# Order of the wide and narrow matmuls in joined products, and joined output tiles 4 to 6 in the mixers

## The chip, the cores and the metric

The kernel runs on one core of a Trainium2 chip. The metric is the device time of one execution in microseconds (us). Five engines of the core matter: TensorE (PE in the profile; its weight loads are shown apart as PEld), VectorE (DVE), ScalarE (ACT), GpSimd (POOL) and SyncE (SP, which issues DMAs). Each works through its instructions in the order in which the program gave them, and semaphores hold an instruction back until its operands are there.

## The reference

The reference is an encoder trunk of four layers over 256 positions of 1024 features. Each layer is a half-step SwiGLU feed-forward network (FFN), a token mixer, and a second FFN, each with a root-mean-square norm ahead of it and behind it:

```python
for i in range(DEPTH):
    g = norm_g[i]
    x = x + 0.5 * rms_norm(swiglu(rms_norm(x, g[0]), ff1_w_in[i], ff1_w_out[i]), g[1])
    h = rms_norm(x, g[2])
    m = mixer_a / mixer_b / mixer_c (h, ...)      # i mod 3
    x = x + rms_norm(m, g[3])
    x = x + 0.5 * rms_norm(swiglu(rms_norm(x, g[4]), ff2_w_in[i], ff2_w_out[i]), g[5])
```

with `swiglu(h) = (silu(gate) * up) @ w_out`, where `gate` and `up` are the halves of `h @ w_in`, of 2816 columns each. Mixer A (layers 0 and 3) is chunked attention with a position bias, mixer B (layer 1) a gated MLP that mixes positions, mixer C (layer 2) differential attention. Each mixer ends in a product with a 1024 x 1024 matrix `w_o`.

## The kernel before

**Numbers in two parts.** Each float32 operand of the large products is held as a high part, rounded to the format that TensorE takes, and a low part, what is left over. A product of weights W and activations X is formed as `Wh*Xh + Wh*Xl + Wl*Xh`. Activations lie transposed (features on the 128 partitions, 256 positions, `S`, along the row), so that a block of 128 x 128 weights times 128 features is a matmul of 256 columns.

**Two ways to multiply.** `product` (L162 to L172) issues three matmuls of 256 columns for each weight block k. `product2` (L174 to L183) takes the high weights against the high and the low activations side by side, one matmul of 512 columns (L177, the wide ones), and then the low weights against the high activations, 256 columns (L179, the narrow ones), which add onto the first half of the same accumulator. All wide matmuls of a call come first, then all narrow ones. A call has eight blocks, or fewer where a weight piece ends inside an output tile. The two halves of the accumulator have to be added afterwards; that is what "joined" means here.

**Where they are used.** An FFN takes its input projection in 11 steps of four weight pieces. The first step has a form of its own (L510 or L529); the other ten call `product2` four times each through `project_apart`. The output product has eight tiles d = 0 to 7 of 22 blocks each; the 22 blocks are cut at the borders of the weight pieces (eight blocks each) into three or four calls. Tiles 0 to 6 use `product2` (25 calls), tile 7 uses `product`. A mixer ends in `project_out`: its tiles 0 to 3 are formed together (L653), tiles 4 to 7 one after the other with `product` (L169), 24 matmuls each. So there are 40 + 25 calls of `product2` in each of the eight FFNs and none in a mixer.

**What happens to an output tile.** `Branch.tile_done` lets ScalarE square the tile (L376, `sq`, or `ysq` for tile 0) and write it times its gain to `yg` (L377); VectorE adds the square to `ysq` (L387). For a joined tile `Branch.joined` comes first: ScalarE copies the second half out of the accumulator (L366, `share`), VectorE adds it to the first half into `yg` (L367), and the square and the gain then read `yg`. After tile 7 TensorE sums the squares over the features (L239): first `ysq` (tiles 0 to 6), then, after four filling matmuls (L449 or L451, early parts of the next stage's first product, by the class `Ahead`), tile 7's `sq`. ScalarE and VectorE make a reciprocal root of it (L247, L249), eight more filling matmuls run beside that, and L254 spreads it over the partitions. Then the residual is updated and the next norm begins. In a mixer the inputs of those filling matmuls that come from `yg` are made late (`YLATE`): three tiles' parts after tile 4 and two after tile 5, each with a ScalarE instruction (L410) and a VectorE instruction (L411).

**The weight stream.** Weights come in pieces of eight blocks, two to a DMA of 1 MB on SyncE's queue, into three buffers. ScalarE rounds a piece to its high part (L127), VectorE subtracts it to get the low part (L130). Eight pieces are held in each form. `W.done` gives a piece back and issues the split of the piece eight further on; a split's VectorE half is issued only with the next split, or by `W.settle`. In a mixer's output one split is issued after tiles 0 to 3 and one after each of the tiles 4, 5 and 6; at tile 7 the stream is held (`W.hold`) until the next norm.

**Order.** The program fixes the order on TensorE, VectorE and ScalarE by hand: it is the order of the calls. Accumulators (`pair()`) come from three pairs of PSUM banks, used in turn.

Of the kernel before, what the change touches and what calls it, by code (L numbers as in the profile page):

```python
# [18 lines left out]
S = 256  # L19
DEPTH = 4  # L20
KD = D // P
# [35 lines left out]
def encoder_trunk_kernel(  # L57
# [14 lines left out]
    nc = tc.nc  # L72
# [90 lines left out]
    W = Stream()  # L163

    def product(o, wh, wl, x, ks, at, start, stop):

        for i, k in enumerate(ks):
            for m, (w_, low) in enumerate(((wh, 0), (wh, 1), (wl, 0))):
                nc.tensor.matmul(  # L169
                    o, w_[:, at + i, :], x(k)[:, low, :], start=(start and i == 0 and m == 0),  # L170
                    stop=(stop and k == ks[-1] and m == 2),
                )  # L172

    def product2(o, wh, wl, x, ks, at, start, stop):  # L174

        for i, k in enumerate(ks):
            nc.tensor.matmul(o, wh[:, at + i, :], x(k), start=(start and i == 0), stop=False, skip_group_check=True)  # L177
        for i, k in enumerate(ks):
            nc.tensor.matmul(  # L179
                o[:, 0:S], wl[:, at + i, :], x(k)[:, 0, :], start=False, stop=(stop and k == ks[-1]),  # L180
                skip_group_check=True,
            )

    def pair():
        return pp.tile([P, 2, 512], F32, tag="pp", name="pp_t")
# [215 lines left out]
    class Ahead:  # L401
# [7 lines left out]
        def parts(self, dst, src, scale):  # L409
            nc.scalar.activation(dst[:, 0, :], src, AF.Copy, scale=scale)  # L410
            nc.vector.scalar_tensor_tensor(  # L411
                dst[:, 1, :], src, scale, dst[:, 0, :].bitcast(F32), op0=ALU.mult, op1=ALU.subtract
            )
# [82 lines left out]
    def blocks(piece):  # L496
        return [part.rearrange("p (k c) -> p k c", k=KD) for part in piece]
# [40 lines left out]
    def project_apart(n, between, finish, most=2):  # L538

        for i in range(4):  # L540
            if i % 2 == 0:
                ps = pair()
            wh, wl = blocks(W.peek())
            product2(ps[:, i % 2, :], wh, wl, lambda k: n.x[:, k], range(KD), 0, True, True)
            if i % 2 == 1:
                finish(i // 2, ps)
            between(i)
            W.done(1, most)
# [93 lines left out]
    def project_out(parts, l, between, ahead):  # L642

        br = Branch(g_sb[:, l, 3, :], None, ahead)
        ws = [blocks(W.peek(e)) for e in range(4)]
        os = [ps[:, e, 0:S] for ps in (pair(), pair()) for e in range(2)]
        for k, low in ORDER:
            if not low:
                between(k)
            x = parts(k)  # L650
            for (wh, wl), o in zip(ws, os):
                for part in (wh,) if low else (wh, wl):
                    nc.tensor.matmul(  # L653
                        o, part[:, k, :], x[:, int(low), :], start=(k == 0 and part is wh and not low),
                        stop=(k == KD - 1 and low), skip_group_check=True,
                    )
            if low and k >= PUMP:
                W.pump(1)
        W.settle()
        for d in range(4):  # L660
            br.tile_done(d, os[d])
        W.done(4, 1)
        for d in range(4, KD):
            o = pair()[:, 0, 0:S]
            wh, wl = blocks(W.peek())
            product(o, wh, wl, parts, range(KD), 0, True, True)
            if d == KD - 1:
                W.hold()
                W.done()
            br.tile_done(d, o)  # L670
            if d < KD - 1:
                W.done(1, 1)
        return br.finish()

    def joined(early, outs):
# [157 lines left out]
    def mixer_a(l, i, update):  # L833
# [86 lines left out]

        late = attention(n, softmax, transposes, v_done, mix)
        return project_out(parts, l, between, ahead)

    def mixer_b(l, i, update):
# [94 lines left out]
        def between(k):  # L1019
# [3 lines left out]
            if k == 3:  # L1023
                split(3)
                nc.scalar.preload_act_table(AF.Sqrt)

        return project_out(lambda k: op[:, k], l, between, ahead)

    def mixer_c(l, i, update):
# [144 lines left out]
        ss = small.tile([P, 16], F32, tag="sso", name="sso", bufs=1)  # L1174
        late = attention(n, softmax, transposes, v_done, mix, prepare, lambda: split(0))
        return project_out(parts, l, between, ahead)

    mixers = (mixer_a, mixer_b, mixer_c)
# [87 lines left out]
```

## Time and profile before

| | |
|---|---|
| Time, median of 3 runs | 1955.42 us (1954.46 to 1955.93) |
| Profiled execution: time, span of its instructions | 1959.09 us, 1957.4 us |
| Mean granted clock of TensorE | 0.997 |
| Wide matmuls of `product2` (L177) | 2560 + 672 + 560 = 3792 |
| Narrow matmuls of `product2` (L179) | 3792 |
| Moved from HBM | 347.44 MB, 178 GB/s over the span |

Times in the profile are those of one profiled execution, from the start of its first instruction. The duration of one matmul includes its way through the array, and the next begins before it has ended: the distance between two starts says more than the duration. The same holds, by about 0.1 us, for instructions of ScalarE and VectorE that stand in a full queue. In rows of the timeline the columns are start, time covered, engine, line, operation, output and inputs, shapes and count; in brackets stands the idle time ahead of it and what ended that.

### The profile page before, as it was taken

Reading aid. Unit: us, or ns where it says so; the run is one execution under the profiler, and the core shown is the slowest. Engines: PE = TensorE matmul, PEld = TensorE weight load, DVE = VectorE, ACT = ScalarE, POOL = GpSimd, SP = SyncE. Lnnn points to the kernel's source line nnn. Section 1 sums busy time; section 2 is a strip of 40 time slices with the busy share of each in tenths; the row PEclk is TensorE's granted clock in tenths of the full one; section 3 lists DMA queues with packets and bytes.
Section 4 is the critical chain, followed back from the end, with each engine's and each line's share of the span. In section 5 each row is a group of like instructions: output and inputs, shape, how many; then the busy total and the mean of one; then the engine's idle time right before and its main releaser. Section 6 shows DMA issues by size and latency. Waiting matters only on the chain.

```text
span 1957.4 us, 30171 instructions
## 1 busy us (share of the span) xinstructions
PE 1941.6 (99%) x12435; PEld 1750.1 (89%) x12435; DVE 1385.1 (71%) x1905; ACT 1177.5 (60%) x1826; POOL 6.7 (0%) x21
## 2 busy tenths in 40 slices
PE   9999999999999999999999999999999999999998
PEld 8888999888988888888988899988898889999887
DVE  6775767866777667867676668786667666868763
ACT  6655657656555555756565655675656565666652
POOL 0000000000000000000000000000000000000000
PEclk9999999999999999999999999999999999999999
DMA  7555534654455553554455535255546454535551
GB/s 260 201 187 200 188 108 153 233 188 180 173 194 188 199 158 147 207 196 177 159 207 190 198 145 181 109 196 194 191 151 214 176 204 159 197 125 182 200 201 44
DMA packets 50473, 350.43 MB, mean 179 GB/s; under 512 B 5760, under 2 KB 6016, under 8 KB 9120
## 3 DMA queue, kind: packets, MB, share of 16 engines
q1 hardware_dynamic: 48096, 341.86, 48.9%
q10 hardware_dynamic: 2160, 6.52, 0.9%
q8 instruction: 97, 1.59, 0.3%
q0 software_dynamic: 80, 0.13, 0.0%
q14 instruction: 40, 0.33, 0.0%
HBM read 347.44 MB, written 1.05 MB: 178 GB/s over the span
## 4 chain that ended last, share of the span: by engine, by line
PE 97%; DVE 1%; DMA 1%; ACT 0%; issue 0%; ACTq 0%; SPq 0%; DVEq 0%
PE pp_t L177 45%; PE pp_t L179 23%; PE pp_t L529 8%; PE pp_t L169 6%; PE pp_t L510 3%; PE pp_t L694 3%; PE pp_t L653 2%; DMA w_raw<-in_w 1%; PE pp_t L734 1%; PE pp_t L451 1%; PE pst_t L766 1%; PE pst_t L451 1%; PE pst_t L239 1%; PE pst_t L254 1%; PE pp_t L449 0%; PE pp_t L888 0%
## 5 line engine op out<-in xcount | busy, mean ns | idle before, releaser
L130 DVE TENSOR_TENSOR w_lo<-w_raw,w_hi 128x1024 fp32r<-128x1024 f32 (+1 forms) x649 | 774.7, 1217 | 57.9 <-ACT w_hi L127 57.8
L127 ACT CAST w_hi<-w_raw 128x1024 fp32r<-128x1024 f32 (+1 forms) x649 | 667.6, 1046 | 122.4 <-PE pp_t L177 84.1
L177 PE MATMUL pp_t<-xp,w_hi 128*128 128x512 f32 x2560 | 642.5, 393 | 0.0
L177 PEld LDWEIGHTS pp_t<-xp,w_hi 128*128 128x128 f32 x2560 | 460.2, 189 | 82.4
L179 PEld LDWEIGHTS pp_t<-xp,w_lo 128*128 128x128 f32 x2560 | 349.2, 190 | 25.1
L179 PE MATMUL pp_t<-xp,w_lo 128*128 128x256 f32 x2560 | 356.8, 282 | 0.0
L600 DVE TENSOR_TENSOR gu<-pp_t,share 128x512 f32<-128x512 f32 x160 | 110.6, 691 | 209.4 <-ACT share L599 209.3
L599 ACT COPY share<-pp_t 128x512 f32<-128x512 f32 x160 | 93.5, 585 | 179.3 <-PE pp_t L179 179.3
L177 PE MATMUL pp_t<-h,w_hi 128*128 128x512 f32 x672 | 175.7, 393 | 0.0
L177 PE MATMUL pp_t<-l,w_hi 128*128 128x512 f32 x560 | 148.8, 394 | 0.0
L570 ACT ACTIVATE gs<-gs 128x512 f32<-128x512 f32 x88 | 55.7, 632 | 141.0 <-DVE gs L569 141.0
L177 PEld LDWEIGHTS pp_t<-h,w_hi 128*128 128x128 f32 x672 | 117.7, 189 | 17.9
L529 PE MATMUL pp_t<-xp,w_hi 128*128 128x256 f32 x832 | 124.3, 288 | 1.7 <-ACT xp L315 1.4
L177 PEld LDWEIGHTS pp_t<-l,w_hi 128*128 128x128 f32 x560 | 100.0, 189 | 20.1 <-DVE l L579 2.9
L529 PEld LDWEIGHTS pp_t<-xp,w_hi 128*128 128x128 f32 x832 | 111.5, 193 | 4.2 <-ACT xp L315 1.6
L179 PEld LDWEIGHTS pp_t<-h,w_lo 128*128 128x128 f32 x672 | 97.7, 190 | 10.3
L367 DVE TENSOR_TENSOR yg<-pp_t,share 128x256 f32<-128x256 f32 x56 | 23.8, 424 | 110.3 <-ACT share L366 110.3
L179 PE MATMUL pp_t<-h,w_lo 128*128 128x256 f32 x672 | 100.6, 282 | 0.0
L179 PEld LDWEIGHTS pp_t<-l,w_lo 128*128 128x128 f32 x560 | 79.6, 190 | 6.1
L179 PE MATMUL pp_t<-l,w_lo 128*128 128x256 f32 x560 | 84.8, 282 | 0.0
L315 ACT ACTIVATE xp<-xr,g_sb 128x256 fp32r<-128x256 f32 x96 | 44.8, 503 | 58.6 <-DVE xr L482 56.5
L529 PE MATMUL pp_t<-xp,w_lo 128*128 128x256 f32 x416 | 73.8, 284 | 0.0
(198 smaller groups left out, 2297.3 us busy)
## 6 DMA issues: line engine op xcount, KB each, us to landing
w_raw<-in_w SPq DMA_DIRECT2D x322, 1024.0 KB, 4.8
l<-in_a_bias ACTq DMA_DIRECT2D x8, 512.0 KB, 8.8
w_raw<-in_w SPq DMA_DIRECT2D x3, 512.0 KB, 8.8
out_y<-xr SPq DMA_DIRECT2D x4, 256.0 KB, 2.1
xr<-in_x_t SPq DMA_DIRECT2D x2, 384.0 KB, 7.0
w_raw<-in_w SPq DMA_DIRECT2D x2, 256.0 KB, 4.7
l<-in_b_ws ACTq DMA_DIRECT2D x1, 512.0 KB, 5.4
l<-in_b_ln_g ACTq DMA_DIRECT2D x1, 512.0 KB, 9.3
```

Of the source, the lines that this page charges most:

```text
L127: nc.scalar.copy(hi[:, cols], raw[:, cols])
L130: nc.vector.tensor_tensor(lo[:, cols], raw[:, cols], hi[:, cols].bitcast(F32), op=ALU.subtract)
L169: nc.tensor.matmul(o, w_[:, at + i, :], x(k)[:, low, :], start=(start and i == 0 and m == 0), stop=(stop and k == ks[-1] and m == 2),)
L177: nc.tensor.matmul(o, wh[:, at + i, :], x(k), start=(start and i == 0), stop=False, skip_group_check=True)
L179: nc.tensor.matmul(o[:, 0:S], wl[:, at + i, :], x(k)[:, 0, :], start=False, stop=(stop and k == ks[-1]), skip_group_check=True,)
L315: nc.scalar.activation(self.h[:, k, :], xr[:, k, :], AF.Copy, scale=gain[:, k:k + 1])
L510: nc.tensor.matmul(o, part[:, k, :], n.x[:, k, int(low), :], start=((k, low) == JOIN[0] and i == 2 and part is ws[i][0]), stop=((k, low) = ...
L529: nc.tensor.matmul(o, part[:, k, :], n.x[:, k, low, :], start=(at == 0), stop=(at == 3 * KD - 1))
L570: nc.scalar.activation(gs, gs, AF.Silu)
L599: nc.scalar.copy(share, ps[:, :, S:2 * S])
L600: nc.vector.tensor_tensor(at.t[:, e], ps[:, :, 0:S], share, op=ALU.add)
L694: nc.tensor.matmul(self.ps[:, t, :], xs[:, kk, t * P:(t + 1) * P], ws, start=((kk, low) == self.order[0] and ws is wh and not (t == 0 and ...
```

## The change

`product2` keeps a switch that turns with every call. One call issues its wide matmuls (high weights) first and its narrow ones (low weights) after, as before; the next issues the narrow ones first and the wide ones after. The flags that begin and end the accumulation go to whichever matmul is first and last. In `project_out` tiles 4, 5 and 6 are formed by `product2` and finished by `joined`; tile 7 stays with `product`.

```diff
+    turn = [False]
+
     def product2(o, wh, wl, x, ks, at, start, stop):
-        for i, k in enumerate(ks):
-            nc.tensor.matmul(o, wh[:, at + i, :], x(k), start=(start and i == 0), stop=False, skip_group_check=True)
-        for i, k in enumerate(ks):
-            nc.tensor.matmul(
-                o[:, 0:S], wl[:, at + i, :], x(k)[:, 0, :], start=False, stop=(stop and k == ks[-1]),
-                skip_group_check=True,
-            )
+        turn[0] = not turn[0]
+        for low in (False, True) if turn[0] else (True, False):
+            for i, k in enumerate(ks):
+                nc.tensor.matmul(
+                    o[:, 0:S] if low else o, (wl if low else wh)[:, at + i, :], x(k)[:, 0, :] if low else x(k),
+                    start=(start and i == 0 and low != turn[0]), stop=(stop and k == ks[-1] and low == turn[0]),
+                    skip_group_check=True,
+                )
...
         for d in range(4, KD):
-            o = pair()[:, 0, 0:S]
+            o = pair()[:, 0, :]
             wh, wl = blocks(W.peek())
-            product(o, wh, wl, parts, range(KD), 0, True, True)
-            if d == KD - 1:
+            if d < KD - 1:
+                product2(o, wh, wl, parts, range(KD), 0, True, True)
+                br.joined(d, o)
+                W.done(1, 1)
+            else:
+                product(o[:, 0:S], wh, wl, parts, range(KD), 0, True, True)
                 W.hold()
                 W.done()
-            br.tile_done(d, o)
-            if d < KD - 1:
-                W.done(1, 1)
+                br.tile_done(d, o[:, 0:S])
```

## The prediction

> **What bounds the kernel now.** I read the page first: busy shares, granted clock, the chain that ended last, the costliest groups.
>
> ```profile
> PE 1941.6 (99%) x12435; PEld 1750.1 (89%) x12435; DVE 1385.1 (71%) x1905; ACT 1177.5 (60%) x1826; POOL 6.7 (0%) x21
> ...
> PEclk9999999999999999999999999999999999999999
> ...
> PE 97%; DVE 1%; DMA 1%; ACT 0%; issue 0%; ACTq 0%; SPq 0%; DVEq 0%
> ...
> L177 PE MATMUL pp_t<-xp,w_hi 128*128 128x512 f32 x2560 | 642.5, 393 | 0.0
> ...
> L179 PE MATMUL pp_t<-xp,w_lo 128*128 128x256 f32 x2560 | 356.8, 282 | 0.0
> ```
>
> TensorE is the chain and its matmuls follow each other without a gap, so what counts is the distance from start to start, not the 393 and 282 ns, which overlap. The chain in order of time gives it.
>
> ```profile
> 34.57 1.84 PE pp_t L177 x8
> ...
> 137.93 1.84 PE pp_t L177 x8
> ...
> 202.51 8.84 PE pp_t L694 x39
> ...
> 299.68 11.52 PE pp_t L169 x96
> ```
>
> Unmixed runs: 8.84/39 = 0.2267 us for 512 columns, 11.52/96 = 0.1200 us for 256. Eight of each would be 2.773 us. The first two rows are the first and last of 38 evenly spaced products: (137.93 - 34.57)/37 = 2.7935 us. So a product pays **0.020 us** for going from one width to the other and back. The timeline shows on which side:
>
> ```profile
> 61.39 1.12 PE L179 MATMUL pp_t<-xp,w_lo 128*128 128x256 f32 x8
> ...
> 62.34 2.00 PE L177 MATMUL pp_t<-xp,w_hi 128*128 128x512 f32 x8
> ...
> 64.19 1.11 PE L179 MATMUL pp_t<-xp,w_lo 128*128 128x256 f32 x8
> ```
>
> Start to start, eight wide ones take 1.85 us instead of 1.81, eight narrow ones 0.95 instead of 0.96.
>
> **The change, part 1: the order in `product2`.** It runs 40 + 25 times per FFN, 520 times in all. With every other call begun low, two calls share one round trip: half of them go. By piece lengths 14 of an FFN's 25 output calls are full and 11 short (2, 4 or 6 blocks); so 432 full calls at 0.020, and 88 short ones at half that by my choice (0 to 0.020 possible): 9.5 us of switching, of which **-4.7 us** goes (-4.3 to -5.2).
>
> A call begun low needs the low weights 1.8 us earlier, but pieces are split eight ahead, over 20 us; and it frees the high half up to 0.95 us later, for which ScalarE's next split waits. Behind that split on ScalarE stands a `share` copy that waits for a product's end anyway, and three PSUM pairs give it two more pairs' time: nothing. One small wait shrinks, in the third output call of each FFN:
>
> ```profile
> 140.56 1.77 PE L177 MATMUL pp_t<-l,w_hi 128*128 128x512 f32 x6
> 142.16 0.40 PE L179 MATMUL pp_t<-l,w_lo 128*128 128x256 f32 x2
> ```
>
> Six take 1.60 us, 0.21 over 6 x 0.231: they wait for the last hidden blocks' low part. By the parity of the calls (65 in an FFN, 3 now in a mixer) the four FFNs of layers 1 and 3 begin this call low, and reach that part later: 4 x 0.21 = 0.8 at most, 0 if their narrow matmuls wait instead; I take **-0.4**.
>
> **Part 2: tiles 4 to 6 of the four mixers.** TensorE saves 2.88 - 2.79 = 0.09 us on each, 0.28 per mixer. But each tile's result now takes ScalarE `share`, VectorE add, ScalarE square, ScalarE scale one after the other. The FFN's output shows these:
>
> ```profile
> 143.13 0.37 ACT L366 COPY share<-pp_t 128x256 f32<-128x256 f32 x1 [0.43 <-PE pp_t L179]
> ...
> 143.54 0.42 DVE L367 TENSOR_TENSOR yg<-pp_t,share 128x256 f32<-128x256 f32 x1 [0.53 <-ACT share L366]
> ...
> 144.00 0.42 ACT L376 ACTIVATE ysq<-yg 128x256 f32<-128x256 f32 x1 [0.49 <-DVE yg L367]
> ...
> 144.45 0.51 ACT L377 ACTIVATE yg<-yg,g_sb 128x256 f32<-128x256 f32 x1
> 144.86 0.49 ACT L410 ACTIVATE ahead<-xr,g_sb 128x256 fp32r<-128x256 f32 x1
> ```
>
> 1.73 us of ScalarE's order. Hidden in an FFN, where a tile is 22 blocks long; a mixer's has 8. ScalarE there, mixer of layer 0:
>
> ```profile
> 301.98 1.10 ACT L127 CAST w_hi<-w_raw 128x1024 fp32r<-128x1024 f32 x1
> 302.91 0.45 ACT L376 ACTIVATE sq<-pp_t 128x256 f32<-128x256 f32 x1
> ...
> 303.55 1.38 ACT L410 ACTIVATE ahead<-yg,g_sb 128x256 fp32r<-128x256 f32 x3
> 304.75 1.11 ACT L127 CAST w_hi<-w_raw 128x1024 fp32r<-128x1024 f32 x1
> 305.68 0.46 ACT L376 ACTIVATE sq<-pp_t 128x256 f32<-128x256 f32 x1
> ...
> 306.31 0.99 ACT L410 ACTIVATE ahead<-yg,g_sb 128x256 fp32r<-128x256 f32 x2
> 307.12 1.12 ACT L127 CAST w_hi<-w_raw 128x1024 fp32r<-128x1024 f32 x1
> 308.36 0.38 ACT L376 ACTIVATE sq<-pp_t 128x256 f32<-128x256 f32 x1
> ...
> 309.00 1.05 ACT L127 CAST w_hi<-w_raw 128x1024 fp32r<-128x1024 f32 x1
> 311.24 0.38 ACT L376 ACTIVATE sq<-pp_t 128x256 f32<-128x256 f32 x1 [1.19 <-PE pp_t L169]
> ```
>
> No idle from tile 0 to tile 6: it is full, and has only 0.3 us before tile 6's square (308.36; the cast ended its turn at 308.05) and 1.3 before tile 7's (311.24; 309.93). Today square and scale take 0.64 (302.91 to 303.55); new, 1.09 more per tile, 1.14 with the somewhat later end of an instruction in a full queue. VectorE adds to it:
>
> ```profile
> 305.36 1.22 DVE L130 TENSOR_TENSOR w_lo<-w_raw,w_hi 128x1024 fp32r<-128x1024 f32 x1
> ...
> 307.74 1.22 DVE L130 TENSOR_TENSOR w_lo<-w_raw,w_hi 128x1024 fp32r<-128x1024 f32 x1
> 308.87 0.41 DVE L387 TENSOR_TENSOR ysq<-ysq,sq 128x256 f32<-128x256 f32 x1
> 309.21 2.35 DVE L130 TENSOR_TENSOR w_lo<-w_raw,w_hi 128x1024 fp32r<-128x1024 f32 x2
> ```
>
> The adds of tiles 5 and 6 stand behind a weight split, moved with the rest. Tile 4: the cast of 304.75 comes 1.14 later, at 305.89. Tile 5: `share` at 306.83 could let the add go at 307.25, but the split of 305.36, now 306.47, holds VectorE to 307.60: 1.14 + 0.33, and the cast of 307.12 comes at 309.72. Tile 6: `share` at 310.65; the split of 307.74 holds VectorE from 310.29 to 311.43, again about 0.32 lost; the add ends at 311.85, square at 312.30, the cast of 309.00 comes at 312.74, tile 7's square at 313.67, **2.43 late**. TensorE, after tile 7:
>
> ```profile
> 311.04 0.50 PE L239 MATMUL pst_t<-ones,ysq 128*128 128x1 f32 x4
> ...
> 311.96 0.50 PE L239 MATMUL pst_t<-ones,sq 128*128 128x1 f32 x4
> ```
>
> It comes to the first sums at 310.76 and waits for tile 6's square sum (today 308.87, then about 312.32 to 312.75): start 312.78, 1.9 us idle. Everything behind waits in TensorE's order: four filling matmuls, then the second sums, which need tile 7's square: 313.67 + 0.48 = 314.15 instead of 311.96, **2.19 late** with the 0.28 already in it. Reciprocal and spread follow at their old distances, TensorE has no idle time later to make it up. Without the VectorE delays (0.65) it is 1.5; with another 0.1 per tile 2.5. The splits that come later are of pieces used only after the next norm, and SyncE's next loads, which wait for them, feed pieces behind those: nothing. All four mixers look alike; the last one's tile 7:
>
> ```profile
> 1757.38 0.38 ACT L376 ACTIVATE sq<-pp_t 128x256 f32<-128x256 f32 x1 [1.19 <-PE pp_t L169]
> ```
>
> 4 x 2.19 = **+8.8 us** (6.0 to 10.0).
>
> **Part 3: the clock.** Such a wait may cost clock as well. Stretches of 3.41 us: busy time and instructions of PE, PEld, DVE, ACT and POOL, then the granted clock (1.00 or 0.50), DMA share and GB/s:
>
> ```profile
> 726.62:730.03 3.41, 2.09 (x18) 1.96 (x17) 2.56 (x5) 3.39 (x5) 0.00 (x0) 1.00 0.94 392
> ...
> 733.45:736.86 3.41, 1.10 (x8) 0.73 (x6) 3.41 (x4) 1.83 (x3) 0.00 (x0) 1.00 0.71 293
> 736.86:740.28 3.42, 1.58 (x6) 1.35 (x6) 3.38 (x4) 0.69 (x1) 0.00 (x0) 0.50 0.00 0
> 740.28:743.69 3.41, 3.32 (x16) 3.25 (x16) 3.41 (x6) 2.19 (x3) 0.00 (x0) 0.50 0.80 288
> ```
>
> After a stretch busy for 2.09 it stayed, after one busy for 1.10 it halved. Halved for one full stretch, TensorE did 16 matmuls instead of 3.41/0.12 = 28: 12.4 x 0.12 = 1.5 us lost. The new waits (1.9 and 0.45, with 0.9 of light work between) leave a stretch busy for 1.1 to 2.1, as it happens to lie. I take two falls in four: **+3.0** (0 to 6.0). The Trainium skill ("TensorE: Matmul & The Clock Gate", Part 1) asks for a whole idle window of about 3.4 us before the clock falls; by that these waits cost none, and the sum would be 3.0 lower. The stretch from 733.45, busy for a third and followed by 0.50, speaks against so strict a reading.
>
> Sum: -4.7 - 0.4 + 8.8 + 3.0 = +6.7. The profiled execution spans 1957.4 us (1959.1 timed), the runs' median is 1955.4; I carry the difference over: **1962 us**.
>
> **Rivals.** *No fall of the clock*: +3.7, 1959. For it: no wait fills a stretch; against: the row of 1.10.
> *The width order saves nothing*: the 0.020 us belongs to the start of a product, not to the switch. Then +8.8 - 0.2 and 0 to 3 for the clock, 1964 to 1967. Against: the 96 matmuls of L169 contain four products and run at 0.1200 throughout. The Trainium skill (same page, Part 1) states a fixed cost for each warm matmul of columns/2.4 plus about 2.5 ns, whatever its neighbours, by which reordering would save nothing; the 2.7935 against 2.773 disagrees.
> *Faster*: ScalarE has 0.3 + 1.3 us of slack and TensorE 0.3 before the second sums. If a tile costs ScalarE under 0.7 us more (the copy's own turn, about 0.3, and the scale's 0.15, with the add beside other work), the tails cost nothing and TensorE keeps 4 x 0.28: -6.2, 1949. Decided at about 0.7 per tile; against it stands that the square waits for the add in ScalarE's order, 0.87 from share to square in the rows above.
>
> **How the numbers follow.** Forecast with one to four falls 0.55 (1959.5 to 1966), no fall 0.2 (1957 to 1960.5), no saving from order 0.1, tails mostly covered 0.15 (two thirds of it faster, the rest near zero). A measurement tells 0.2% apart, 3.9 us: slower is above 1959.3, faster below 1951.5. The slower cases hold 0.55 + 0.1 less a little, same the no-fall case and a third of the last: faster 0.10, same 0.28, slower 0.62. Range 1954 to 1967.
>
> **What would show it.** Right: periods alternating about an average of 2.784 us; TensorE idle near 1.9 us before L239 in four places, released by VectorE's `ysq` sum, and 0.4 by ScalarE's `sq`; stretches at 0.50 after them. Wrong: tile 7's square still idle-waiting for TensorE, or periods still 2.7935.

## The result, and the profile after

| | median, us | lowest to highest | runs |
|---|---|---|---|
| before | 1956.64 | 1954.46 to 1958.79 | 6 |
| changed | 1968.68 | 1966.37 to 1972.09 | 6 |

The changed kernel takes 1.006 of the time before, 95% interval 1.005 to 1.007: **12 us slower**, where 1962 was forecast (some 7 us more than the median shown then) with a range up to 1967. Its profiled execution took 1970.4 us, over a span of 1968.6.

The page of the changed kernel; `product2` is now one line, L183, and the sums after tile 7 are L244:

```profile
span 1968.6 us, 29946 instructions
...
PE 1946.6 (99%) x12339; PEld 1756.1 (89%) x12339; DVE 1391.3 (71%) x1917; ACT 1183.5 (60%) x1838; POOL 6.8 (0%) x21
...
PEclk9999999999999998999999999999999999999999
...
PE 94%; DVE 3%; ACT 2%; DMA 1%; issue 0%; ACTq 0%; SPq 0%; DVEq 0%
```

TensorE's share of the chain falls from 97% to 94%; VectorE holds 3% of it (1% before) and ScalarE 2% (0%), and the clock has a slice below 9. The waits of TensorE say where:

```profile
PE pst_t L244 <- DVE ysq L392: 7.3, 4, 1.8
```

Four waits of 1.8 us, one in each mixer, which were not there before. ScalarE in the tail of layer 0's mixer, timeline of the changed kernel; the rows to set beside these are those of 301.98 to 311.24 before (this stretch begins 1.0 us earlier now):

```profile
301.87 0.44 ACT L371 COPY share<-pp_t 128x256 f32<-128x256 f32 x1
302.80 0.42 ACT L381 ACTIVATE sq<-yg 128x256 f32<-128x256 f32 x1 [0.49 <-DVE yg L372]
...
304.87 1.03 ACT L127 CAST w_hi<-w_raw 128x1024 fp32r<-128x1024 f32 x1
305.80 0.36 ACT L371 COPY share<-pp_t 128x256 f32<-128x256 f32 x1
306.98 0.42 ACT L381 ACTIVATE sq<-yg 128x256 f32<-128x256 f32 x1 [0.82 <-DVE yg L372]
...
308.65 1.03 ACT L127 CAST w_hi<-w_raw 128x1024 fp32r<-128x1024 f32 x1
309.59 0.36 ACT L371 COPY share<-pp_t 128x256 f32<-128x256 f32 x1
310.76 0.42 ACT L381 ACTIVATE sq<-yg 128x256 f32<-128x256 f32 x1 [0.82 <-DVE yg L372]
...
312.56 0.37 ACT L381 ACTIVATE sq<-pp_t 128x256 f32<-128x256 f32 x1
```

VectorE at the same place:

```profile
305.40 1.22 DVE L130 TENSOR_TENSOR w_lo<-w_raw,w_hi 128x1024 fp32r<-128x1024 f32 x1
306.54 0.41 DVE L372 TENSOR_TENSOR yg<-pp_t,share 128x256 f32<-128x256 f32 x1
...
309.18 1.22 DVE L130 TENSOR_TENSOR w_lo<-w_raw,w_hi 128x1024 fp32r<-128x1024 f32 x1
310.31 0.42 DVE L372 TENSOR_TENSOR yg<-pp_t,share 128x256 f32<-128x256 f32 x1
```

In the brackets one reads ScalarE standing still for 0.49 us at tile 4 and 0.82 at tiles 5 and 6, each time until the add; at tiles 5 and 6 VectorE did the weight split first. Tile 7's square comes at 312.56; the place before, moved by the 1.0, would be 310.2. TensorE (the last row has two of its four matmuls, since the view ends there):

```profile
311.69 0.61 PE L244 MATMUL pst_t<-ones,ysq 128*128 128x1 f32 x4 [1.81 <-DVE ysq L392]
...
312.99 0.59 PE L244 MATMUL pst_t<-ones,sq 128*128 128x1 f32 x2
```

So far this is the forecast to about a tenth of a us. What is new is the clock. Stretches of 3.41 us of the changed kernel behind the mixers of layers 0 and 1 (columns as in the prediction, the clock is the 1.00 or 0.50):

```profile
309.03:312.44 3.41, 1.60 (x14) 1.39 (x13) 2.93 (x5) 2.56 (x5) 0.00 (x0) 1.00 0.16 41
312.44:315.86 3.42, 3.42 (x17) 3.27 (x16) 1.64 (x3) 1.12 (x4) 0.00 (x0) 0.50 0.88 309
315.86:319.27 3.41, 3.41 (x18) 3.41 (x17) 2.36 (x6) 1.01 (x2) 0.00 (x0) 0.50 0.63 264
...
776.66:780.07 3.41, 2.70 (x21) 2.49 (x21) 2.87 (x4) 2.44 (x6) 0.00 (x0) 1.00 0.90 300
780.07:783.48 3.41, 3.41 (x19) 3.41 (x18) 2.23 (x6) 1.02 (x2) 0.00 (x0) 0.50 0.89 291
```

It fell behind all four mixers, for two stretches in layers 0 and 2 and for one in layers 1 and 3. Taking the same landmarks of both traces (the reciprocals of the norms), each tail and what follows it to the next norm costs 5.0, 4.0, 5.0 and 3.7 us, 17.7 in all; the FFNs give 4.7 back; the stall at the start of mixer B is 1.1 shorter and the first FFN begins 0.8 earlier, both where weights are waited for. These last two need not be the change's: the profiled execution of the kernel before was 2.5 us above its median.

### The profile page after: what moved, and what is told of

It is laid out like the page before. It is cut to its first block, busy times and chain, and to the rows that moved or that the text cites. A ratio compares the mean times of both kernels' runs of the same rounds, so it can differ in the third digit from the quotient of the medians.

```text
span 1968.6 us, 29946 instructions
## 1 busy us (share of the span) xinstructions
PE 1946.6 (99%) x12339; PEld 1756.1 (89%) x12339; DVE 1391.3 (71%) x1917; ACT 1183.5 (60%) x1838; POOL 6.8 (0%) x21
## 4 chain that ended last, share of the span: by engine, by line
PE 94%; DVE 3%; ACT 2%; DMA 1%; issue 0%; ACTq 0%; SPq 0%; DVEq 0%
PE pp_t L183 67%; PE pp_t L534 8%; PE pp_t L169 4%; PE pp_t L515 3%; PE pp_t L701 3%; PE pp_t L658 2%; DMA w_raw<-in_w 1%; PE pp_t L741 1%; PE pp_t L456 1%; PE pst_t L456 1%; DVE w_lo L130 1%; PE pst_t L244 1%; PE pst_t L773 1%; PE pst_t L259 1%; DVE ahead L416 1%; ACT yg L382 1%
## 5 line engine op out<-in xcount | busy, mean ns | idle before, releaser
L183 PE MATMUL pp_t<-xp,w_hi 128*128 128x512 f32 x2560 | 613.7, 391 | 0.0
L183 PEld LDWEIGHTS pp_t<-xp,w_hi 128*128 128x128 f32 x2560 | 469.7, 188 | 90.4
L183 PEld LDWEIGHTS pp_t<-xp,w_lo 128*128 128x128 f32 x2560 | 329.0, 191 | 12.5
L183 PE MATMUL pp_t<-xp,w_lo 128*128 128x256 f32 x2560 | 334.6, 283 | 0.0
L183 PE MATMUL pp_t<-h,w_hi 128*128 128x512 f32 x708 | 178.1, 391 | 0.0
L183 PEld LDWEIGHTS pp_t<-h,w_hi 128*128 128x128 f32 x708 | 128.6, 189 | 23.8
L183 PE MATMUL pp_t<-l,w_hi 128*128 128x512 f32 x584 | 149.1, 392 | 0.0
L183 PEld LDWEIGHTS pp_t<-l,w_hi 128*128 128x128 f32 x584 | 106.8, 188 | 21.8 <-DVE l L584 1.6
L534 PEld LDWEIGHTS pp_t<-xp,w_hi 128*128 128x128 f32 x832 | 111.4, 193 | 3.6 <-ACT xp L320 1.0
L372 DVE TENSOR_TENSOR yg<-pp_t,share 128x256 f32<-128x256 f32 x68 | 28.8, 423 | 105.8 <-ACT share L371 105.8
L183 PEld LDWEIGHTS pp_t<-h,w_lo 128*128 128x128 f32 x708 | 95.9, 191 | 5.2
L183 PE MATMUL pp_t<-h,w_lo 128*128 128x256 f32 x708 | 100.3, 283 | 0.0
L183 PE MATMUL pp_t<-l,w_lo 128*128 128x256 f32 x584 | 84.5, 283 | 0.0
L183 PEld LDWEIGHTS pp_t<-l,w_lo 128*128 128x128 f32 x584 | 78.9, 191 | 3.1
L534 PE MATMUL pp_t<-xp,w_lo 128*128 128x256 f32 x416 | 73.8, 284 | 0.0
```

The costliest lines, as they stand in the source:

```text
L183: nc.tensor.matmul(o[:, 0:S] if low else o, (wl if low else wh)[:, at + i, :], x(k)[:, 0, :] if low else x(k), start=(start and i == 0 and ...
L534: nc.tensor.matmul(o, part[:, k, :], n.x[:, k, low, :], start=(at == 0), stop=(at == 3 * KD - 1))
```

## The experiments

All are compared with the kernel before, run on the same chip among them. The mean clock is that of all timed runs of a kernel; before it is 0.997.

| run | median, us | before, us | ratio (95%) | mean clock |
|---|---|---|---|---|
| e1_order_only | 1952.19 | 1957.33 | 0.9977 (0.9967 to 0.9986) | 0.9970 |
| e2_joined_only | 1968.85 | 1957.33 | 1.0066 (1.0053 to 1.0078) | 0.9950 |
| e3_filler_in_wait | 1962.82 | 1957.33 | 1.0027 (1.0016 to 1.0038) | 0.9970 |
| e4_split_beside_add | 1969.64 | 1957.33 | 1.0063 (1.0050 to 1.0076) | 0.9926 |
| e5_order_and_tile4 | 1953.21 | 1957.33 | 0.9981 (0.9972 to 0.9989) | 0.9972 |
| e6_low_split_behind_add | 1955.82 | 1957.33 | 0.9993 (0.9984 to 1.0001) | 0.9967 |
| e7_thin_filler | 1970.08 | 1957.33 | 1.0065 (1.0051 to 1.0079) | 0.9922 |
| e8_order_low_third | 1952.19 | 1957.33 | 0.9976 (0.9967 to 0.9985) | 0.9975 |
| e9_thin_filler_88 | 1967.69 | 1956.62 | 1.0058 (1.0045 to 1.0071) | 0.9930 |
| e10_changed_again | 1968.26 | 1956.62 | 1.0067 (1.0054 to 1.0081) | 0.9920 |

**The two parts of the change, each alone.** The first keeps the new `product2` and puts the old loop back in `project_out`:

```diff
         for d in range(4, KD):
-            o = pair()[:, 0, :]
+            o = pair()[:, 0, 0:S]
             wh, wl = blocks(W.peek())
-            if d < KD - 1:
-                product2(o, wh, wl, parts, range(KD), 0, True, True)
-                br.joined(d, o)
-                W.done(1, 1)
...
+            product(o, wh, wl, parts, range(KD), 0, True, True)
```

> The alternating order alone; the mixers' tiles 4 to 6 as before. Theory A (the order saves 4.7 us, all the loss sits in the mixers' tails): about 1951.5 us against 1956.5 of before, no wait at L244 (the sums after tile 7), no stretch at half clock there. Rival B (the alternating order itself makes work late, since low weights are needed earlier and high slots come free later): 1957 us or more, with new waits of TensorE inside the FFNs.

The second keeps the new loop and puts the old `product2` back.

> Joined tiles 4 to 6 in the mixers alone, product2 in its old order. Theory A: the whole loss without the gain, 1956.5 + 17 = about 1973 us, with a wait of 1.9 to 2.0 us before the sums in each of four mixers and one or two stretches of 3.41 us at half clock behind each. Rival B: the joined tiles are harmless, 1955 to 1957 us.

The order alone is 5.1 us faster than before, with no wait at the sums and the clock as before: the harm is not in it (rival B of the first run falls). The joined tiles alone are 11.5 us slower, with the four waits: rival B of the second falls too.

```profile
PE pst_t L239 <- DVE ysq L387: 7.2, 4, 1.8
```

They cost 4 us less than expected, and their clock is higher (0.9950 against 0.9925). So the two parts do not add up to the change: -5.1 and +11.5 make +6.4, where +12 was measured. The missing 5 us or so are what the difference in clock stands for, at the 2 us for a thousandth that e10 shows below. Why the clock falls more often, or for longer, with both parts together is not shown; where the limits of the stretches lie beside the tails differs from profile to profile.

**Is it the clock?** Fifteen matmuls of a constant tile are put where TensorE waits; the lateness stays and the idle time goes.

```diff
                 self.ss = bank()
+                if not self.n:
+                    self.ahead.begin()
+                    for _ in range(15):
+                        nc.tensor.matmul(self.ahead.ps[:, 1, 0:S], filler[:, 0:P], filler, start=True, stop=True)
                 column_sums(self.ss, self.acc, True, False)
...
```

> The changed kernel with 15 matmuls of a constant tile put ahead of the first sums of a mixer, where TensorE waits; they compute nothing that is used. Theory A1 (the wait costs 2.05 us per mixer and the clock's fall another 9.4 us in all): the squares stay as late as they were, the clock stays at 1.00, 1968.7 - 9 = about 1959.5 us. Rival A2 (the half clock is not caused by the idle time): the clock falls all the same, 1968 us or more.

The time falls from 1968.68 to 1962.82 and the clock is back at 0.997. The first stretch over a mixer's tail and the one after it, in this run:

```profile
311.00:314.41 3.41, 3.12 (x26) 2.55 (x24) 2.93 (x5) 2.59 (x6) 0.00 (x0) 1.00 0.59 195
314.41:317.82 3.41, 3.41 (x31) 3.41 (x31) 2.29 (x7) 0.98 (x3) 0.00 (x0) 1.00 0.85 310
```

Between its landmarks each tail is now 2.18 us late (2.8 in mixer B, which had begun otherwise), with nothing added behind it. Counting mixer B like the others, the late squares alone cost 8.7 us in the four mixers and the clock the rest. By the medians the late squares cost more: this run is 5.5 us above before although the order saves 5.1, 10.6 in all. The clock's part can be had twice as well: 5.9 us between the medians, and (0.9970 - 0.9925) x 1957 = 8.8 us from the mean clocks, since a missing thousandth of clock stands for twice a thousandth of the time at half clock, half of which is lost. The medians have an uncertainty of some 3 us, so these runs put the late squares at 9 to 11 us and the clock at 6 to 9. The time came out 3 us above the expected 1959.5; the order's gain and four tails of 2.18 would give 1960.9, within what the intervals allow.

**What makes the clock fall?** Thin matmuls occupy TensorE without streaming columns:

```diff
-                    for _ in range(15):
-                        nc.tensor.matmul(self.ahead.ps[:, 1, 0:S], filler[:, 0:P], filler, start=True, stop=True)
+                    for _ in range(24):
+                        nc.tensor.matmul(self.ahead.ps[:, 1, 0:8], filler[:, 0:P], filler[:, 0:8], start=True, stop=True)
```

> The changed kernel with 24 matmuls of 8 columns in the wait instead of 15 of 256 columns; they compute nothing that is used. TensorE is then occupied with instructions for most of the wait, but streams next to no columns. Theory A3 (the clock follows the columns that are streamed in a stretch of 3.41 us: it fell after shares of 0.39 and less and stayed after 0.44 and more): it falls as in the changed kernel, 1967 to 1970 us. Rival A4 (the clock follows the time without an instruction): it stays, about 1963 us as with the wide filler.

1970.08 us, clock 0.992: it fell, in the profile behind three of the four mixers. But the 24 took only 0.8 us, and 1.2 us of idle time were left. With 88 of them nothing is left:

> As the run with the thin filler, but with 88 matmuls of 8 columns, since 24 took only 0.5 us of the 2 us of waiting: about 1.8 us of instructions that stream 0.3 us worth of columns; they compute nothing that is used. Theory A3 (the clock follows the columns streamed): two to four of the four mixers fall to half clock, 1966 to 1970 us. Rival A4 (it follows the time without an instruction): none falls, about 1963 us as with the wide filler.

The timeline of that run, and two of its stretches:

```profile
310.03 2.35 PE L388 MATMUL pp_t<-filler 128*128 128x8 bf16 x88
312.25 0.58 PE L244 MATMUL pst_t<-ones,ysq 128*128 128x1 f32 x4
...
314.98 0.41 PE L460 MATMUL pp_t<-ahead,w_lo 128*128 128x256 f32 x1
315.19 0.63 PE L460 MATMUL pp_t<-ahead,w_hi 128*128 128x256 f32 x2
315.62 0.41 PE L460 MATMUL pp_t<-ahead,w_lo 128*128 128x256 f32 x1
```

```profile
309.54:312.95 3.41, 3.41 (x100) 3.37 (x99) 2.93 (x5) 2.56 (x6) 0.00 (x0) 1.00 0.34 77
312.95:316.36 3.41, 3.41 (x18) 3.41 (x18) 1.46 (x3) 0.94 (x4) 0.00 (x0) 0.50 0.80 279
```

A stretch in which TensorE is busy from end to end, with 100 matmuls, is followed by 0.50: three of the four mixers fell, as A3 said. So neither idle time nor TensorE's busy time decides; what the wide filler brings and the thin one does not are columns. At 0.50 three matmuls of 256 columns take 315.62 - 314.98 = 0.64 us, 0.213 each, so 0.107 at full clock. With that I worked out, from the recorded starts, for every stretch of the changed kernel and of e2, e3 and e4 which share of its 3.41 us the matmuls' columns would fill at full clock. Behind the mixers, shares of 0.14 to 0.38 were followed by half clock; once the kernel is under way none of 0.46 or more was (the filler brings it to 0.46 to 0.48). The other profiles narrow this: the clock also stayed after 0.41 and 0.42 (e6, e7, e10).

The border is not sharp by this reckoning: in e5 a stretch of 0.36 close to the end kept the full clock. If the columns are taken 0.06 us behind the recorded starts, that stretch comes to 0.38, and then all profiles agree: 0.36 and less fell, 0.38 and more stayed. Much the same border shows in how long it lasts: at half clock a stretch can fill 0.5 at most; behind the mixers, after 0.30 to 0.35 it stayed down for a second stretch, after 0.36 (e9) and 0.41 to 0.45 the full clock came back. In layer 0's tail the one that kept it down held the second sums, 0.88 us of one-column matmuls. The stall at the start of mixer B fits only if its matmuls of 128 columns count as 256: with their columns as they are, a stretch of 0.31 at half clock was enough there (e1, e6, e8); counted double it is 0.39 to 0.41. They start 0.112 us apart at full clock, nearly as far as matmuls of 256 columns, but that they count so is an assumption.

The changed kernel once more, on that chip:

> The changed kernel again, beside the thin filler on the same chip, to see how its time goes with the time at half clock. Theory: 1966 to 1972 us, and 0.001 less of mean clock costs about 2 us (half of the 3.9 us at half clock that it stands for).

Its five runs went from 1967.3 us at a clock of 0.993 to 1973.4 at 0.990: 2 us for a thousandth, as expected, which accounts for the spread of this kernel's runs. In its profile mixer B's tail escaped, at a share of 0.42, and only layer 0 had two stretches at half clock: four in all, against six in the first profile. By the landmarks one stretch cost 1.5 us and two cost 2.8, in both profiles.

**What makes the squares late?** First, ScalarE's split of the next piece is moved into the time in which ScalarE waits for the add; the VectorE half of the split before it is held back (`defer`) and put behind the tile (`settle_older`; both are additions to the stream that are left out here):

```diff
             nc.vector.tensor_tensor(self.yg[:, d, :], o[:, 0:S], share, op=ALU.add)
+            split()
             self.tile_done(d, self.yg[:, d, :])
...
-                br.joined(d, o)
-                W.done(1, 1)
+                W.defer = True
+                br.joined(d, o, lambda: W.done(1, 1))
+                W.settle_older()
```

> The changed kernel, but in tiles 4 to 6 ScalarE's split of the next weight piece stands between the copy of the second half and the square, where ScalarE waits for VectorE's add, and the split's VectorE half stands behind the tile. Theory A (ScalarE's order, with 1.1 us more per tile and 0.33 where VectorE is busy, makes tile 7's square 2.4 us late): the wait before the sums falls from 2.0 to about 0.5 us, no half clock, about 1953 us. Rival C (the added latency of share, add and square is what counts, wherever the split stands): a wait of over 1.5 us stays, over 1960 us.

1969.64 us, no gain: the wait is 2.2 us. My expectation failed, and VectorE's timeline in this run shows why:

```profile
304.87 1.22 DVE L134 TENSOR_TENSOR w_lo<-w_raw,w_hi 128x1024 fp32r<-128x1024 f32 x1
306.01 0.41 DVE L382 TENSOR_TENSOR yg<-pp_t,share 128x256 f32<-128x256 f32 x1
...
308.65 1.22 DVE L134 TENSOR_TENSOR w_lo<-w_raw,w_hi 128x1024 fp32r<-128x1024 f32 x1
309.79 0.42 DVE L382 TENSOR_TENSOR yg<-pp_t,share 128x256 f32<-128x256 f32 x1
```

ScalarE's copy of tile 5 was ready at 304.69, but the add still follows the split. From add to add it is 3.78 us, and TensorE makes a tile in 2.79: the two engines hand the tile to and fro, and moving one side's work shifts the bound to the other. So the VectorE half of the split before goes right behind the add as well, where VectorE waits for the square (against the run just shown):

```diff
-                W.defer = True
                 br.joined(d, o, lambda: W.done(1, 1))
-                W.settle_older()
```

> As the run with the split beside the add, but the VectorE half of the split before stands right behind the add too, so that the next tile's add no longer waits for it. Theory D (in that run VectorE's order took over: add, square sum, two or three ahead parts, split, next add, 3.78 us per tile where TensorE needs 2.79): the wait before the sums falls from 2.2 to about 0.7 us, the clock stays, about 1954 us. Rival C (the latency of a joined tile counts, wherever the splits stand): a wait of over 1.5 us stays, 1965 us or more.

```profile
PE pst_t L244 <- DVE ysq L393: 2.8, 4, 0.7
```

VectorE's adds of tiles 5 and 6 in this run:

```profile
306.40 0.42 DVE L372 TENSOR_TENSOR yg<-pp_t,share 128x256 f32<-128x256 f32 x1
306.74 1.22 DVE L130 TENSOR_TENSOR w_lo<-w_raw,w_hi 128x1024 fp32r<-128x1024 f32 x1
...
309.29 0.42 DVE L372 TENSOR_TENSOR yg<-pp_t,share 128x256 f32<-128x256 f32 x1
```

From add to add it is 2.89 us. The wait shrinks to 0.7 us, the clock stays, 1955.82 us, 2 above the expected 1954. Theory D holds, C falls: the place of the splits makes most of the wait, not the latency of a joined tile by itself. What is left of it, 2.8 us in the four mixers, still makes this run 3.6 us slower than the order alone.

Last, tile 4 alone joined, on top of the new order:

> The alternating order, and of the mixers' tiles only tile 4 joined. Theory A: ScalarE's 1.1 us more at tile 4 fits into its slack of 0.3 + 1.3 us, so no wait before the sums, no half clock behind a mixer, and TensorE keeps 0.09 us per mixer: 0.3 to 0.4 us below the order alone, about 1951.8 us. Rival C (each joined tile in a mixer costs its part of the 2 us): about 0.7 us of wait per mixer, 1955 us.

No wait, clock as before: one joined tile fits into the slack. But 1953.21 against 1952.19 for the order alone is no difference that these runs can tell, and the 0.3 us hoped for cannot be seen.

**The third output call.** In the order alone, the turn is set so that this call begins low in every FFN:

```diff
         br = Branch(g_sb[:, l, 4 * which + 1, :], n, ahead)
+        turn[0] = True
         b = 0
```

> The alternating order alone, with the turn set at the start of every FFN's output product so that its third call begins with the low weights in all eight FFNs. Theory: the 0.2 to 0.27 us that the third call waits in four of the FFNs goes there too, about 1 us below the order alone, 1951 us; rival: that wait is only moved, 1952 us.

The small wait is gone in all eight FFNs, and the time is 1952.19 again; the landmarks of both profiles give 4.7 us for the eight FFNs. It came back elsewhere, because the edit turns another call too: with 25 calls behind a fixed turn, every FFN's input projection now begins high, and its second call low. In the second FFN of each layer that second call waits. This run there:

```profile
325.97 1.22 DVE L130 TENSOR_TENSOR w_lo<-w_raw,w_hi 128x1024 fp32r<-128x1024 f32 x1
326.63 0.50 PE L244 MATMUL pst_t<-ones,sqacc 128*128 128x1 f32 x4
327.24 1.21 PE L183 MATMUL pp_t<-xp,w_lo 128*128 128x256 f32 x8
```

And the order alone:

```profile
326.74 0.50 PE L244 MATMUL pst_t<-ones,sqacc 128*128 128x1 f32 x4
327.10 1.65 PE L183 MATMUL pp_t<-xp,w_hi 128*128 128x512 f32 x6
```

The low matmuls start 0.61 us behind the sums' start instead of 0.36, 0.05 us after VectorE has ended a split (325.97 + 1.22 = 327.19); that is so in all four, which points to this split as what they wait for. It is 0.25 us in each of four FFNs, about what the four third calls gained.

The order alone is the version that beats both kernels; with the turn set, or with tile 4 joined, it is as fast as far as these runs can tell.

## Why the prediction was wrong

- **The order of the widths**: forecast -4.7 and -0.4, measured -5.1 in e1; that the sum fits so well is in part luck, since the interval is -2.7 to -6.5. In the profile of e1 the excess of all of `product2`'s matmuls over 0.2267 and 0.1200 us falls by 4.7 us, some 0.5 of it in the third call, so switching itself gave about 4.2. The short calls, which I had put at half price, did pay less before (two wide ones in a row 0.016 us instead of 0.027); now no run is shorter than eight, and all pay the full price. That the low weights are always there in time held in the changed kernel, but not in e8. In the changed kernel's chain one piece shows the new average:

```profile
28.18 111.82 PE pp_t L183 x642
```

  642 matmuls are 40.1 products: 2.787 us each, against 2.7935 before and 2.784 forecast. The rival that the order saves nothing is refuted. So is, as far as mixed widths go, the even cost of each matmul that the Trainium skill gives ("TensorE: Matmul & The Clock Gate", Part 1).
- **The late squares**: forecast 1.9 us idle and 2.19 late in each mixer; measured 1.81 idle, and 2.18 late where the clock stayed (e3). ScalarE's and VectorE's orders and the adds behind the splits came as worked out. The second wait, for tile 7's square, shows where the clock stayed: in e3 the second sums start 1.30 us behind the first, 0.92 before. The rival in which the tails are covered needed under 0.7 us more per tile; from `share` to the instruction behind the tile's scale it was 1.80 to 2.05 us, where square and scale took 0.64 before, so 1.2 to 1.4 more.
- **The clock**, the step that failed: "I take two falls in four". That such a wait costs clock was right, and so was the price, 1.5 us for a stretch at half clock; how many stretches there would be was not. All four mixers fell in the profile of the changed kernel, two of them for two stretches: six stretches where two were forecast, about 9 us by the landmarks (17.7 less 4 x 2.18), 8.8 by the mean clocks of the six runs and 6 between the medians, where +3.0 was forecast. Two things were wrong in it. I measured a stretch by TensorE's busy time; but 776.66:780.07 was busy for 2.70 us and was followed by half clock, because eight of its 21 matmuls have one column. And I let a fall last one stretch, while two of four lasted two. My upper bound of 6.0, four falls of one stretch, therefore was none, and 1967 was too low. The forecast change was +6.7, the measured one +12.0: the clock makes 3 to 6 of the difference, and what is left of it lies in the late squares, whose size the runs put at 9 to 11. That the medians of before came out 1.2 us higher than the ones shown moved the time as well. That no fall would come, as the Trainium skill's rule of a whole idle window that the prediction cites has it, is refuted by e9, where no stretch is idle.

## What to carry to other kernels

Joining tiles to save matmuls is paid on the engines that take the result over: count their order per tile against TensorE's time per tile, with the wait of each engine for the other, before the last tile whose sum everything waits for. A wait of TensorE has a second price where it leaves a stretch of the clock's measure too thin; here wide matmuls of a constant in the gap kept that away, and thin ones did not. Alternating which width comes first keeps half of the switches out, and is free where the low weights are there in time for a call that begins with them.

## What the runs showed of the hardware

- In these profiles the clock falls to half behind a stretch of 3.41 us in which the matmuls' columns fill less than some 0.37 of it at full clock (0.36 and less fell, 0.38 and more stayed, by the reckoning above), however busy TensorE is with instructions: e9 has 100 matmuls in 3.41 us, a share of 0.26, and falls. At half clock much the same border decides about the return, so a stretch that is two thirds full at half clock (0.33) keeps it down. The stretches are 3.41 us long, as the Trainium skill has it ("TensorE: Matmul & The Clock Gate", Part 1). That the border lies at columns and not at idle time is not what that section says.
- Going from 256 to 512 columns costs the first five matmuls together 0.027 us, going back gains 0.007, before and in e1 alike; from six wide ones on the length of the runs between does not matter.
- A square of `yg` and the scaled copy of `yg` onto itself behind it start 0.45 us apart on ScalarE (302.80 and 303.25), after the first has ended; two instructions that read the accumulator stand 0.28 us apart (312.56 and 312.84). Why is not shown.
